# Norm scratch in PSUM, the context's norm first, and other banks for the feed-forward's opening, in a two-layer fp32 transformer kernel

## The chip, the cores and the metric

One core of a Trainium2 chip runs the whole program in one launch. The metric is the device time of that core in microseconds (us); lower is better.

## The reference, cut to what matters

Two layers over 512 latent tokens and 256 context tokens, 1024 features, fp32. Each layer has a mixer (layer 0: mLSTM heads and windowed attention; layer 1: global and neighbourhood attention) and a convolutional feed-forward, and in front of each stands a modulated RMS norm:

```python
def rms_norm(x, g):
    y = xf * lax.rsqrt(jnp.mean(xf * xf, axis=-1, keepdims=True) + EPS)
    return (y * g.astype(f32)).astype(x.dtype)

def modulate(x, g, shift, scale):
    return rms_norm(x, g) * (1 + scale) + shift

def conv_ffn(h, w_up, conv_w, conv_b, w_down):
    u = h @ w_up                                   # 1024 -> 2 x 2816
    u = depthwise_conv3(u, conv_w) + conv_b
    gate, val = jnp.split(u, 2, axis=-1)
    return (jax.nn.silu(gate) * val) @ w_down
```

Mixer and feed-forward are added to x through gates. Latents and context have their own shift, scale and gate. Of layer 1 only the latent stream is an output, so its second norm and its feed-forward see 512 tokens.

## The kernel before, in words

x lies transposed in SBUF: 8 tiles j of 128 features by 768 tokens (512 latent, 256 context). A matrix product is made from split operands: weight and activation are each rounded to a high half (fp32r, a faster matmul type) plus a low remainder, and three matmuls (high by high, high by low, low by high) add up in PSUM; `mm3` (L164 to L174) writes them out, `gemm_set` (L303) does the same with tokens on the output's partitions. Every weight block goes through `wchunk` (L138): SyncE issues a DMA of up to 512 KB into one of 4 "raw" buffers, ScalarE rounds it to `whi` (L145), GpSimd subtracts to get `wlo` (L146); there are 3 buffers of each.

PSUM has eight banks of 512 fp32 columns, handed out by tag (L69): "s" two buffers of two banks, "t" two of one bank, "mm" and "o" one each. `mmps` (L73) takes the tags in `mmtags` in turn. The order of instructions on each engine is fixed when the program is built: instructions are traced in program order and a list scheduler with a simulated timeline orders each engine's queue; on the chip each queue runs in that order and waits at semaphores.

A norm other than the first has these steps, on one stream of n tokens (512, or 256):

- behind each output tile of a projection, VectorE updates x (L1046 in `out_proj`, L1154 in the feed-forward's down product), ScalarE squares the new tile into an SBUF buffer `sq` (two buffers, L247), and VectorE adds it to `acc` (L248, both operands in SBUF)
- `norm_stat` (L250): matmuls by a column of ones sum `acc` over features into a "t" bank (L258); `rsqrt` (L120) computes 1/rms with twelve small VectorE instructions (L125 to L132), all but the first in SBUF; matmuls against the identity broadcast it to all partitions into another "t" bank (L265); ScalarE copies that to SBUF `rb` (L267)
- `norm_tile` (L271), for each of 8 j: VectorE scales x by weight and 1/rms into `ntmp` (four SBUF buffers, L279), ScalarE adds the shift and rounds to the high half (L281), VectorE makes the low half (L282). The halves are `hlh`, `hll` for latents and `hch`, `hcl` for context.

Three places have such norms. In `run` (L1166) layer 0's second norm: the second half of the output projection on latents, their norm, the same projection on the context, its norm, then `ffn`. At the end of `ffn` for layer 0 the last down product runs for latents, then for the context, and each stream's norm (layer 1's first) follows; `odd_mixer` then opens with a product by `W2` whose four latent token tiles run side by side in both "s" buffers (`wide`, L321). Layer 1's second norm treats the 512 latents as two halves of 256 with a projection each; the first half's high and low parts go to the context's tiles H[2], H[3], and DMAs move them later.

`ffn` (L1051) opens with the first four output tiles, (0,0), (0,1), (1,0), (1,1): for the first stream all four tiles, then for the second, so that TensorE has work while the second stream is normed. In layer 0 stream 0 is latents (512 columns), stream 1 context. Their banks are "s", "mm" with half of "o", "s", "t" with the other half of "o"; in layer 1 "s", "s", "mm", "o". The fourth tile's weights use spare buffers of later gate tiles.

Of the kernel before, what the change touches and what calls it, by code (L numbers as in the profile page):

```python
# [6 lines left out]
F32 = mybir.dt.float32  # L7
# [8 lines left out]
P = 128  # L16
# [13 lines left out]
NB0, NB1, NB2 = (2, 2), (2, 4), (2, 4)  # L30
# [13 lines left out]
class Net:  # L44
# [194 lines left out]
    def sq_acc(self, pool, acc, x, first, pool_add=False):  # L239

        nc = self.nc
        if first:
            nc.scalar.activation(acc, x, AF.Square)
        else:
            n = x.shape[-1]
            sq = pool.tile([P, 512], F32, tag="sq", bufs=self.nb[0], name=self.n("sq"))
            nc.scalar.activation(sq[:, :n], x, AF.Square)  # L247
            (nc.gpsimd if pool_add else nc.vector).tensor_tensor(acc, acc, sq[:, :n], op=ALU.add)  # L248

    def norm_stat(self, pool, *accs, tags=("t", "t")):  # L250
# [11 lines left out]
        for (acc, n), t0 in zip(accs, at):  # L262
# [3 lines left out]
            rb = pool.tile([P, 512], F32, tag="rb", bufs=2, name=self.n("rb"))  # L266
            nc.scalar.activation(rb[:, :n], bp[:, :n], AF.Copy)  # L267
            rbs.append(rb)
        return rbs

    def norm_tile(self, pool, l, i, j, X, rb, t0, n, s, hh, hl, o0):  # L271
# [3 lines left out]
        tm = pool.tile([P, 512], F32, tag="ntmp", bufs=self.nb[1], name=self.n("ntmp"))  # L275
        a, b, c = tm[:, :n], X[:, j, t0:t0 + n], rb[:, :n]
# [4 lines left out]
        nc.scalar.activation(hh[:, j, o0:o0 + n], tm[:, :n], AF.Identity, bias=sh)  # L281
        nc.vector.scalar_tensor_tensor(hl[:, j, o0:o0 + n], tm[:, :n], sh, hh[:, j, o0:o0 + n], op0=ALU.add, op1=ALU.subtract)  # L282

    def norm_apply(self, pool, l, i, X, acc, t0, n, s, hh, hl, o0):
        rb, = self.norm_stat(pool, (acc, n))
        for j in range(KT):
            self.norm_tile(pool, l, i, j, X, rb, t0, n, s, hh, hl, o0)
# [32 lines left out]

    def wide(self):  # L321

        s2 = [self.psum("s") for _ in range(2)]
        return [(t, s2[t // 2][:, t % 2 * 512:t % 2 * 512 + 512]) for t in range(NLT)]
# [291 lines left out]
    def start(self, X, H, pool, ev_gate, room):  # L616
# [19 lines left out]
        for i, (a, b) in enumerate(((0, LAT), (LAT, TOK))):  # L636
            got = set()
            for j in range(KT):
                h = int(i == 0 and j in (1, 3))
                self.sq_acc(pool, sums[i][h], X[:, j, a:b], h not in got, h)  # L640
                got.add(h)
            if len(got) > 1:
                nc.vector.tensor_tensor(sums[i][0], sums[i][0], sums[i][1], op=ALU.add)
            rbs += self.norm_stat(pool, (sums[i][0], b - a), tags=(("t", "t"), ("mm", "o"))[i])
# [4 lines left out]
        for j in range(KT):  # L649
            ada(j + AHEAD)  # L650
            for (t0, n, s) in ((0, LAT, 0), (LAT, CTX, 1)):
                self.norm_tile(pool, 0, 0, j, X, rbs[s], t0, n, s, H[2 * s], H[2 * s + 1], 0)
# [11 lines left out]
    def even_mixer(self, es):  # L664
# [26 lines left out]
        with ExitStack() as ns:  # L691
            self.nrm = self.pool("nrm0", ns)
            self.nb = NB0
# [165 lines left out]
    def odd_mixer(self, H, xd, es):  # L859
# [38 lines left out]
        self.mmtags = ["mm", "t"]  # L898
        wk = outer.tile([P, 2, 1024], F32R, tag="nq", name="wk")
        W2 = self.chunks(W[2], 256, self.K2)  # L900
        self.gemm_set(W2, 256, self.wide(), H, ev(ckv, 0, 1))
# [126 lines left out]
    def out_proj(self, l, ksel, xin, xout, streams, accs):  # L1028

        nc, d = self.nc, self.d  # L1030
        for jp in range(4):
# [8 lines left out]
            for jj in range(2):  # L1040
                j = 2 * jp + jj
                for i, (hh, hl, o0, n, t0, s) in enumerate(streams):
# [4 lines left out]
                    if accs is not None:  # L1047
                        self.sq_acc(self.nrm, accs[i], xs, j == 0)


    def ffn(self, l, X, H, T, tail, es, fin=None, work=None):  # L1051
# [6 lines left out]
        def banks(j, half):  # L1058

            if lat_only:  # L1060
                u = self.psum("s" if j != 1 else ("mm", "o")[half])[:, :LAT]
# [40 lines left out]
        for gi, (p0, p1) in enumerate(GROUPS):  # L1102
            G = []
            ready = {}
            if gi == 0:
                first = [(0, 0), (0, 1), (1, 0), (1, 1)]
                Ws = [weights(*f, spare=i == 3) for i, f in enumerate(first)]
                if lat_only:
                    us = [banks(*f) for f in first]
                else:  # L1110
                    o = self.psum("o")
                    us = [banks(0, 0), [self.psum("mm")[:, :LAT], o[:, :CTX]], banks(1, 0), [self.psum("t")[:, :LAT], o[:, CTX:]]]
                for i in range(2):
# [5 lines left out]
            for j in range(p0, p1):  # L1119
                cv = []  # L1120
                for half in range(2):
                    u = ready.get((j, half))
                    if u is None:
                        W = weights(j, half)
# [17 lines left out]
            for streams in passes:  # L1142
                for j in range(KT):
# [6 lines left out]
                    for o0, n, t0, s, acc in cut:  # L1150
# [4 lines left out]
                        if acc is not None:  # L1155
                            self.sq_acc(self.nrm, acc, xs, j == 0)
# [9 lines left out]
    def run(self):  # L1166
# [6 lines left out]
        self.nb = NB1  # L1173
# [3 lines left out]
        xj = lambda j: X[:, j, :]  # L1177
# [125 lines left out]
```

## Time and profile before, and how to read it

| | |
|---|---|
| time, median of 3 runs | 1817.64 us (1816.6 to 1818.77) |
| the profiled execution's own time | 1819.8 us |
| its span, first to last instruction | 1818.0 us |
| mean granted clock of TensorE | 0.985 |
| busy: TensorE, VectorE, ScalarE, GpSimd | 1713.1, 892.2, 659.0, 682.9 us |

In the profile PE is TensorE, DVE VectorE, ACT ScalarE, POOL GpSimd, SP SyncE. Times are us from the start of the span unless marked ns; L279 is line 279 of the kernel before; `out<-in` are the program's names; `x7` counts instructions. A row of waits names the engine and line that stood idle and the engine and line that released it. The granted clock is the share of full speed that TensorE was given.

### The profile page before, as it was taken

Reading aid. Unit: us, or ns where it says so; the run is one execution under the profiler, and the core shown is the slowest. Engines: PE = TensorE matmul, PEld = TensorE weight load, DVE = VectorE, ACT = ScalarE, POOL = GpSimd, SP = SyncE. Lnnn points to the kernel's source line nnn. Section 1 sums busy time; section 2 is a strip of 40 time slices with the busy share of each in tenths; the row PEclk is TensorE's granted clock in tenths of the full one; section 3 lists DMA queues with packets and bytes.
Section 4 is the critical chain, followed back from the end, with each engine's and each line's share of the span. In section 5 each row is a group of like instructions: output and inputs, shape, how many; then the busy total and the mean of one; then the engine's idle time right before and its main releaser. Section 6 shows DMA issues by size and latency. Waiting matters only on the chain.

```text
span 1818.0 us, 27843 instructions
## 1 busy us (share of the span) xinstructions
PE 1713.1 (94%) x11057; PEld 1461.1 (80%) x11057; DVE 892.2 (49%) x1897; ACT 659.0 (36%) x1145; POOL 682.9 (38%) x539
## 2 busy tenths in 40 slices
PE   4899998899899999999999988899989799999999
PEld 4679788788688888888788878789867788888887
DVE  6642458775853321333134477776266854143242
ACT  3422343553443311322123343365445444243341
POOL 2133226443422222222323353644374534443442
PEclk9999999999899999999999998999999899999999
DMA  8542431401323333332431242211242333323322
GB/s 294 177 171 70 155 130 52 132 22 36 105 70 105 128 105 128 105 125 99 136 129 55 73 163 70 71 42 36 73 128 74 124 98 102 93 92 86 113 86 77
DMA packets 62257, 187.62 MB, mean 103 GB/s; under 512 B 8048, under 2 KB 14320, under 8 KB 61872
## 3 DMA queue, kind: packets, MB, share of 16 engines
q1 hardware_dynamic: 62128, 185.85, 32.1%
q8 instruction: 87, 1.43, 0.3%
q14 instruction: 42, 0.34, 0.1%
HBM read 170.68 MB, written 4.39 MB: 96 GB/s over the span
## 4 chain that ended last, share of the span: by engine, by line
PE 81%; DVE 11%; ACT 2%; POOL 2%; DMA 2%; issue 1%; SPq 0%; DVEq 0%; ACTq 0%; POOLq 0%
PE s L170 11%; PE s L172 11%; PE s L174 11%; PE mm L170 3%; PE mm L172 3%; PE mm L174 3%; PE t L170 3%; PE o L603 3%; PE t L172 3%; PE t L174 3%; PE t L583 3%; PE o L170 2%; PE o L174 2%; PE o L172 2%; PE mm L310 2%; PE o L186 2%
## 5 line engine op out<-in xcount | busy, mean ns | idle before, releaser
L146 POOL TENSOR_TENSOR wlo<-raw,whi 128x1024 fp32r<-128x1024 f32 (+2 forms) x210 | 492.0, 2348 | 881.7 <-ACT whi L145 855.4
L145 ACT ACTIVATE whi<-raw 128x1024 fp32r<-128x1024 f32 (+2 forms) x210 | 214.2, 1025 | 503.7 <-PE s L172 179.0
L172 PE MATMUL s<-hll,whi 128*128 128x512 f32 (+1 forms) x704 | 275.9, 392 | 4.8 <-DVE hll L282 4.8
L170 PE MATMUL s<-hlh,whi 128*128 128x512 f32 (+1 forms) x704 | 277.2, 394 | 2.9 <-ACT hlh L281 2.6
L174 PE MATMUL s<-hlh,wlo 128*128 128x512 f32 (+1 forms) x704 | 275.5, 391 | 0.0
L1096 DVE SCALAR_TENSOR_TENSOR cv<-s,convw,cv 128x511 f32<-128x511 f32 x126 | 82.9, 658 | 330.1 <-ACT cv L1090 330.0
L170 PEld LDWEIGHTS s<-hlh,whi 128*128 128x128 f32 x704 | 132.6, 188 | 48.9 <-ACT whi L145 10.1
L172 PEld LDWEIGHTS s<-hll,whi 128*128 128x128 f32 x704 | 132.8, 189 | 33.8 <-DVE hll L282 5.4
L174 PEld LDWEIGHTS s<-hlh,wlo 128*128 128x128 f32 x704 | 132.6, 188 | 30.3 <-issue 0.8
L567 POOL TENSOR_SCALAR P<-P,sm 128x512 f32<-128x512 f32 (+3 forms) x112 | 84.0, 755 | 110.4 <-DVE sm L566 80.6
L172 PE MATMUL s<-hcl,whi 128*128 128x256 f32 x384 | 109.3, 285 | 5.6 <-DVE hcl L282 5.6
L174 PE MATMUL s<-hch,wlo 128*128 128x256 f32 x384 | 108.4, 282 | 0.0
L170 PE MATMUL s<-hch,whi 128*128 128x256 f32 x384 | 108.1, 282 | 0.0
L310 PE MATMUL mm<-whi,hlh 128*128 128x256 f32 x312 | 92.0, 295 | 4.0 <-ACT l1xt L876 2.4
L311 PE MATMUL mm<-wlo,hlh 128*128 128x256 f32 x312 | 90.1, 289 | 0.0
L312 PE MATMUL mm<-whi,hll 128*128 128x256 f32 x312 | 89.7, 287 | 0.0
L583 PE MATMUL t<-ident,P 128*128 128x128 f32 x496 | 77.9, 278 | 9.5 <-POOL E L964 4.7
L170 PE MATMUL t<-gh,whi 128*128 128x512 f32 (+1 forms) x221 | 85.8, 389 | 0.0
L1097 DVE SCALAR_TENSOR_TENSOR cv<-s,convw,cv 128x511 f32<-128x511 f32 x126 | 83.2, 661 | 4.5
L174 PE MATMUL t<-gh,wlo 128*128 128x512 f32 (+1 forms) x221 | 84.8, 384 | 0.0
L172 PE MATMUL t<-gl,whi 128*128 128x512 f32 (+1 forms) x221 | 84.8, 384 | 0.0
L172 PEld LDWEIGHTS s<-hcl,whi 128*128 128x128 f32 x384 | 73.3, 191 | 6.9 <-DVE hcl L282 6.0
(443 smaller groups left out, 4083.9 us busy)
## 6 DMA issues: line engine op xcount, KB each, us to landing
raw<-ada SPq DMA_DIRECT2D x96, 512.0 KB, 4.1
raw<-up SPq DMA_DIRECT2D x86, 512.0 KB, 3.7
raw<-down SPq DMA_DIRECT2D x40, 448.0 KB, 3.4
raw<-wout SPq DMA_DIRECT2D x24, 512.0 KB, 3.6
raw<-wodd SPq DMA_DIRECT2D x18, 512.0 KB, 3.6
raw<-down SPq DMA_DIRECT2D x16, 512.0 KB, 3.6
raw<-wtok SPq DMA_DIRECT2D x12, 512.0 KB, 3.8
raw<-wqk SPq DMA_DIRECT2D x8, 512.0 KB, 4.7
```

Source lines behind the costliest of these rows:

```text
L145: nc.scalar.activation(hi[:, :cols], raw[:, :cols], AF.Copy)
L146: nc.gpsimd.tensor_tensor(lo[:, :cols], raw[:, :cols], hi[:, :cols], op=ALU.subtract)
L170: nc.tensor.matmul(ps, wh, hh(k), start=(k == 0), stop=False, skip_group_check=True)
L172: nc.tensor.matmul(ps, wh, hl(k), start=False, stop=False, skip_group_check=True)
L174: nc.tensor.matmul(ps, wl, hh(k), start=False, stop=(k == nk - 1), skip_group_check=True)
L310: nc.tensor.matmul(ps[:, :ncols], a, W[k][0], start=(k == 0), stop=False, skip_group_check=True)
L311: nc.tensor.matmul(ps[:, :ncols], a, W[k][1], start=False, stop=False, skip_group_check=True)
L312: nc.tensor.matmul(ps[:, :ncols], b, W[k][0], start=False, stop=(k == KT - 1), skip_group_check=True)
L567: nc.gpsimd.tensor_scalar(Pt[:, :n], Pt[:, :n], sm, 0.0, op0=ALU.mult, op1=ALU.add)
L583: nc.tensor.transpose(tp[:, (b - g0) * P:(b - g0 + 1) * P], Pts[e][:, b * P:(b + 1) * P], self.ident)
L1096: nc.vector.scalar_tensor_tensor(y[:, a + 1:b], u[:, 0:n - 1], w(0), y[:, a + 1:b], op0=ALU.mult, op1=ALU.add)
L1097: nc.vector.scalar_tensor_tensor(y[:, a:b - 1], u[:, 1:n], w(2), y[:, a:b - 1], op0=ALU.mult, op1=ALU.add)
```

## The change

The changed functions serve all norms behind the first (the first keeps its SBUF buffers through `keep=True` and arguments). `slots(n)` takes one "s" buffer (two banks) and hands out slices of n columns in turn: two of 512 or four of 256. One such buffer holds the squares of a projection, another the scaled x of a norm, and 1/rms is read by VectorE from the "t" bank of the broadcast, with no copy. In layer 0 the context's projection and norm go ahead of the latents', and the feed-forward opens with three tiles, context stream first, in "mm" with half of "o", "t" with the other half, and "s"; the fourth tile's weights are still loaded there and used when its turn comes. In layer 1 the four opening tiles take "mm", "o", "s", "t". `wide` goes: the odd mixer's first product runs its latent token tiles one after another in banks "mm", "o", "t".

```diff
-    def sq_acc(self, pool, acc, x, first, pool_add=False):
+    def sq_acc(self, acc, x, first, sq, pool_add=False):
         nc = self.nc
         if first:
             nc.scalar.activation(acc, x, AF.Square)
         else:
-            n = x.shape[-1]
-            sq = pool.tile([P, 512], F32, tag="sq", bufs=self.nb[0], name=self.n("sq"))
-            nc.scalar.activation(sq[:, :n], x, AF.Square)
-            (nc.gpsimd if pool_add else nc.vector).tensor_tensor(acc, acc, sq[:, :n], op=ALU.add)
+            nc.scalar.activation(sq, x, AF.Square)
+            (nc.gpsimd if pool_add else nc.vector).tensor_tensor(acc, acc, sq, op=ALU.add)
+
+    def slots(self, n):
+        ps = self.psum("s")
+        return lambda j: ps[:, j % (1024 // n) * n:j % (1024 // n) * n + n]
...
-    def norm_stat(self, pool, *accs, tags=("t", "t")):
+    def norm_stat(self, pool, *accs, tags=("t", "t"), keep=False):
...
-            rb = pool.tile([P, 512], F32, tag="rb", bufs=2, name=self.n("rb"))
-            nc.scalar.activation(rb[:, :n], bp[:, :n], AF.Copy)
-            rbs.append(rb)
+            if keep:
+                rb = pool.tile([P, 512], F32, tag="rb", bufs=2, name=self.n("rb"))
+                nc.scalar.activation(rb[:, :n], bp[:, :n], AF.Copy)
+            rbs.append(rb if keep else bp)
         return rbs
-    def norm_tile(self, pool, l, i, j, X, rb, t0, n, s, hh, hl, o0):
+    def norm_tile(self, l, i, j, X, rb, t0, n, s, hh, hl, o0, tm):
         nc = self.nc
-        tm = pool.tile([P, 512], F32, tag="ntmp", bufs=self.nb[1], name=self.n("ntmp"))
-        a, b, c = tm[:, :n], X[:, j, t0:t0 + n], rb[:, :n]
+        a, b, c = tm, X[:, j, t0:t0 + n], rb[:, :n]
...
     def norm_apply(self, pool, l, i, X, acc, t0, n, s, hh, hl, o0):
         rb, = self.norm_stat(pool, (acc, n))
+        tm = self.slots(n)
         for j in range(KT):
-            self.norm_tile(pool, l, i, j, X, rb, t0, n, s, hh, hl, o0)
+            self.norm_tile(l, i, j, X, rb, t0, n, s, hh, hl, o0, tm(j))
...
-        self.mmtags = ["mm", "t"]
+        self.mmtags = ["mm", "o", "t"]
         wk = outer.tile([P, 2, 1024], F32R, tag="nq", name="wk")
         W2 = self.chunks(W[2], 256, self.K2)
-        self.gemm_set(W2, 256, self.wide(), H, ev(ckv, 0, 1))
+        for t in range(NLT):
+            self.gemm_set(W2, 256, [(t, self.mmps())], H, ev(ckv, 0, 1))
...
     def out_proj(self, l, ksel, xin, xout, streams, accs):
+        sqs = [self.slots(n) for _, _, _, n, _, _ in streams] if accs is not None else None
...
-                        self.sq_acc(self.nrm, accs[i], xs, j == 0)
+                        self.sq_acc(accs[i], xs, j == 0, sqs[i](j))
...
             if lat_only:
-                u = self.psum("s" if j != 1 else ("mm", "o")[half])[:, :LAT]
+                u = self.psum("s")[:, :LAT]
                 return [u[:, a:b] for a, b in segs] + [u]
...
                 Ws = [weights(*f, spare=i == 3) for i, f in enumerate(first)]
+                early = dict(zip(first, Ws))
                 if lat_only:
-                    us = [banks(*f) for f in first]
+                    us = [[u[:, a:b] for a, b in segs] + [u[:, :LAT]] for u in (self.psum(t) for t in ("mm", "o", "s", "t"))]
                 else:
                     o = self.psum("o")
-                    us = [banks(0, 0), [self.psum("mm")[:, :LAT], o[:, :CTX]], banks(1, 0), [self.psum("t")[:, :LAT], o[:, CTX:]]]
-                for i in range(2):
+                    us = [[self.psum("mm")[:, :LAT], o[:, :CTX]], [self.psum("t")[:, :LAT], o[:, CTX:]], banks(1, 0)]
+                for i in ((0, 1) if lat_only else (1, 0)):
                     for W, u in zip(Ws, us):
                         self.mm3(W, [stream(u, i)])
                 ready = dict(zip(first, us))
...
-                        W = weights(j, half)
+                        W = early.pop((j, half), None) or weights(j, half)
...
             for streams in passes:
+                sq = self.slots(streams[0][1]) if streams[0][4] is not None else None
...
-                            self.sq_acc(self.nrm, acc, xs, j == 0)
+                            self.sq_acc(acc, xs, j == 0, sq(j))
...
         al, ac = self.acc(LAT), self.acc(CTX)
         xj = lambda j: X[:, j, :]
+        self.out_proj(0, Bk, xj, xj, [cx], [ac])
+        H = self.htiles()
+        self.norm_apply(self.nrm, 0, 1, X, ac, LAT, CTX, 1, H[2], H[3], 0)
         self.out_proj(0, Bk, xj, xj, [lat], [al])
-        H = self.htiles()
         self.norm_apply(self.nrm, 0, 1, X, al, 0, LAT, 0, H[0], H[1], 0)
-        self.out_proj(0, Bk, xj, xj, [cx], [ac])
-        self.norm_apply(self.nrm, 0, 1, X, ac, LAT, CTX, 1, H[2], H[3], 0)
```

## Rows read from the trace of the kernel before

**Rows 1.** The page, part 1: busy us (share of the span) and instructions of each engine.

```profile
PE 1713.1 (94%) x11057; PEld 1461.1 (80%) x11057; DVE 892.2 (49%) x1897; ACT 659.0 (36%) x1145; POOL 682.9 (38%) x539
```

**Rows 2.** Waits of TensorE, three stretches: line waited for: us, times, longest.

```profile
PE s L172 <- DVE hll L282: 4.5, 1, 4.5
PE t L258 <- DVE acc L248: 2.8, 1, 2.8
PE t L265 <- DVE y L132: 1.8, 1, 1.8
...
PE s L312 <- DVE hll L282: 4.0, 2, 3.6
PE t L265 <- DVE y L132: 3.5, 1, 3.5
PE s L311 <- POOL wlo L146: 2.3, 1, 2.3
...
PE s L172 <- DVE hcl L282: 5.6, 2, 4.4
PE t L258 <- DVE acc L248: 3.5, 1, 3.5
PE s L170 <- ACT hlh L281: 1.5, 1, 1.5
```

**Rows 3.** Stretches: us, busy (instructions) by engine, granted clock, DMA share, GB/s.

```profile
440.00:535.00 95.00, 84.09 (x474) 72.72 (x473) 64.69 (x109) 39.59 (x59) 32.26 (x14) 0.95 0.23 73
1040.00:1125.00 85.00, 73.99 (x505) 68.69 (x504) 63.72 (x99) 32.53 (x53) 37.88 (x17) 0.94 0.37 118
1400.00:1500.00 100.00, 87.40 (x590) 79.72 (x590) 67.24 (x120) 44.15 (x74) 41.38 (x20) 0.93 0.31 102
1064.00:1068.00 4.00, 4.00 (x36) 4.00 (x36) 2.41 (x3) 1.64 (x3) 3.58 (x2) 1.00 1.03 346
```

**Rows 4.** VectorE by shape, 444:500 and 1408:1470: busy us, mean ns, idle before.

```profile
L248 DVE TENSOR_TENSOR acc<-acc,sq 128x512 f32<-128x512 f32 x7 | 11.9, 1697 | 2.0 <-ACT sq L247 1.1 <-ACT acc L243 0.7
L279 DVE SCALAR_TENSOR_TENSOR ntmp<-x,avec,rb 128x512 f32<-128x512 f32 x8 | 9.5, 1222 | 1.0 <-ACT rb L267 1.0
L282 DVE SCALAR_TENSOR_TENSOR hll<-ntmp,mod,hlh 128x512 fp32r<-128x512 f32 x8 | 8.3, 1055 | 0.0
...
L248 DVE TENSOR_TENSOR acc<-acc,sq 128x256 f32<-128x256 f32 x14 | 15.4, 1097 | 1.4 <-ACT sq L247 0.9
...
L282 DVE SCALAR_TENSOR_TENSOR hcl<-ntmp,mod,hch 128x256 fp32r<-128x256 f32 x8 | 7.8, 992 | 0.0
L282 DVE SCALAR_TENSOR_TENSOR hll<-ntmp,mod,hlh 128x256 fp32r<-128x256 f32 x8 | 3.4, 479 | 0.0
```

**Rows 5.** Timeline (start us, us), then one source line (min/median/max ns).

```profile
452.47 2.40 POOL L146 TENSOR_TENSOR wlo<-raw,whi 128x1024 fp32r<-128x1024 f32 x1 [4.73 <-ACT whi L145]
...
453.01 2.41 DVE L248 TENSOR_TENSOR acc<-acc,sq 128x512 f32<-128x512 f32 x1 [0.70 <-ACT acc L243]
...
456.01 0.68 DVE L248 TENSOR_TENSOR acc<-acc,sq 128x512 f32<-128x512 f32 x1
...
1418.03 0.41 DVE L248 TENSOR_TENSOR acc<-acc,sq 128x256 f32<-128x256 f32 x1
...
L1154 DVE SCALAR_TENSOR_TENSOR x<-t,mod,x x30: 468/751/752, 649.6 to 1814.8; 128x512 f32<-128x512 f32 x27, 128x256 f32<-128x256 f32 x3
```

**Rows 6.** 1/rms on VectorE: a group by shape in 1040:1125, then two timeline rows.

```profile
L127 DVE TENSOR_SCALAR y<-ms 128x4 int32<-128x4 int32 x1 | 1.8, 1844 | 0.0
...
1104.26 0.16 DVE L125 TENSOR_SCALAR ms<-t 128x2 f32<-128x2 f32 x1 [1.10 <-PE t L258]
...
1106.43 0.16 DVE L132 SCALAR_TENSOR_TENSOR y<-rt,y 128x2 f32<-128x2 f32 x1
```

**Rows 7.** Timeline of TensorE at layer 1's first broadcast.

```profile
1074.18 1.16 PE L265 MATMUL t<-ident,y 128*128 128x128 f32 x8 [3.54 <-DVE y L132]
1075.10 0.37 PE L170 MATMUL t<-gh,whi 128*128 128x256 f32 x1
```

More of the change, by code (lines that the diff above doesn't have):

```diff
@@ L29 @@
 WR, WH, RB0 = 4, 3, 2
-NB0, NB1, NB2 = (2, 2), (2, 4), (2, 4)
+NB0 = (2, 2)
 PB1, EB, PB0, PTB = 4, 2, 4, 4
@@ L280, in norm_tile @@
         sh = self.modcol(l, 3 * i, j, s)
-        nc.scalar.activation(hh[:, j, o0:o0 + n], tm[:, :n], AF.Identity, bias=sh)
-        nc.vector.scalar_tensor_tensor(hl[:, j, o0:o0 + n], tm[:, :n], sh, hh[:, j, o0:o0 + n], op0=ALU.add, op1=ALU.subtract)
+        nc.scalar.activation(hh[:, j, o0:o0 + n], tm, AF.Identity, bias=sh)
+        nc.vector.scalar_tensor_tensor(hl[:, j, o0:o0 + n], tm, sh, hh[:, j, o0:o0 + n], op0=ALU.add, op1=ALU.subtract)
     def norm_apply(self, pool, l, i, X, acc, t0, n, s, hh, hl, o0):
         rb, = self.norm_stat(pool, (acc, n))
+        tm = self.slots(n)
         for j in range(KT):
-            self.norm_tile(pool, l, i, j, X, rb, t0, n, s, hh, hl, o0)
+            self.norm_tile(l, i, j, X, rb, t0, n, s, hh, hl, o0, tm(j))
     def htiles(self):
@@ L319, in gemm_tok @@
             self.gemm_set(W, ncols, [(t, self.mmps())], H, evac)
-    def wide(self):
-        s2 = [self.psum("s") for _ in range(2)]
-        return [(t, s2[t // 2][:, t % 2 * 512:t % 2 * 512 + 512]) for t in range(NLT)]
     K2 = ((0, 4), (4, 8))
@@ L639, in start @@
                 h = int(i == 0 and j in (1, 3))
-                self.sq_acc(pool, sums[i][h], X[:, j, a:b], h not in got, h)
+                sq = pool.tile([P, 512], F32, tag="sq", bufs=NB0[0], name=self.n("sq")) if h in got else None
+                self.sq_acc(sums[i][h], X[:, j, a:b], h not in got, sq and sq[:, :b - a], h)
                 got.add(h)
@@ L643, in start @@
                 nc.vector.tensor_tensor(sums[i][0], sums[i][0], sums[i][1], op=ALU.add)
-            rbs += self.norm_stat(pool, (sums[i][0], b - a), tags=(("t", "t"), ("mm", "o"))[i])
+            rbs += self.norm_stat(pool, (sums[i][0], b - a), tags=(("t", "t"), ("mm", "o"))[i], keep=True)
         for j in range(AHEAD):
@@ L651, in start @@
             for (t0, n, s) in ((0, LAT, 0), (LAT, CTX, 1)):
-                self.norm_tile(pool, 0, 0, j, X, rbs[s], t0, n, s, H[2 * s], H[2 * s + 1], 0)
+                tm = pool.tile([P, 512], F32, tag="ntmp", bufs=NB0[1], name=self.n("ntmp"))
+                self.norm_tile(0, 0, j, X, rbs[s], t0, n, s, H[2 * s], H[2 * s + 1], 0, tm[:, :n])
             for t in range(NTT):
@@ L692, in even_mixer @@
             self.nrm = self.pool("nrm0", ns)
-            self.nb = NB0
             self.start(X, H, self.nrm, ev_gate, hs)
@@ L1172, in run @@
         self.nrm = self.pool("nrm1", ns)
-        self.nb = NB1
         self.mmtags = ["mm", "o", "t"]
@@ L1199, in run @@
         self.nrm = self.pool("nrm2", ns)
-        self.nb = NB2
         self.mmtags = ["mm", "o", "t"]
```

## The prediction, made before the changed kernel was run

> **What bounds the kernel now.** The page comes first: TensorE is busy for 94% of the span [rows 1], so most of the time is matrix work that this change leaves alone, and what it can win is TensorE's waiting and its slow clock at the three places where a norm stands between two matrix products. The waits of TensorE, asked for each of these stretches, give it: 9.1 us around layer 0's second norm (4.5 + 2.8 + 1.8), 9.8 us around layer 1's first (4.0 + 3.5 + 2.3), 10.6 us around layer 1's second (5.6 + 3.5 + 1.5), 29.5 us in all, and nearly all of it ends with a VectorE instruction of the norm [rows 2]. The stretches by engine show a second loss: the granted clock has a mean of 0.95, 0.94 and 0.93 there, against 1.00 in a stretch without waits [rows 3]. With two levels, 1.2 and 2.4 GHz, a mean of 0.95 over 95 us costs at most 0.05 x 95 = 4.8 us of full-speed work, the others 0.06 x 85 = 5.1 and 0.07 x 100 = 7.0, 16.9 us together; some of it fell on idle time and cost nothing. So 29.5 + 16.9 = 46.4 us is the most that can come back.
>
> Why is VectorE late? The groups by shape show it. Adding a 512-wide square takes 1697 ns in the mean, the scaling 1222, the low part 1055 in layer 0; the first is 680 ns when left alone [rows 4, 5]. The 256-wide low part takes 992 ns in layer 1's second norm for the first half of the tokens and 479 for the second, the same work [rows 4]. The timeline tells the two cases apart: the 2.41 us addition started while GpSimd made a low weight half (2.40 us from 452.47) and ended half a microsecond behind it; the next, with GpSimd idle, took 0.68. And thirty updates of x, the same two-tensor form but with the product read from PSUM, lie between 468 and 752 ns [rows 5], though GpSimd is busy for 38% of the span [rows 1]. So a VectorE instruction with both tensors in SBUF stands still behind GpSimd; one with a tensor in PSUM doesn't.
>
> **Part by part.** *Squares, scaled x and 1/rms in PSUM.* All three two-tensor instructions of a later norm get a PSUM operand. Against the unblocked prices (additions 0.68 at 512 and 0.41 at 256; scaling and low part 0.75, as the update of x, and 0.48) the blocked time is 7 x 1.02 + 8 x 0.47 + 8 x 0.31 = 13.4 us in layer 0, and in layer 1's second norm 14 x 0.69 + 8 x 0.51 = 13.7 without its scalings [rows 4, 5]. That is VectorE's time; TensorE gets back only what it waited for. Six copies of 1/rms by ScalarE go too, each between the broadcast and the first scaling; they stand inside the waits for the low and high parts and are not counted again.
>
> No row shows VectorE or ScalarE writing to PSUM. The nearest is the update of x, which reads it at the SBUF price (468 against 479 ns at 256) [rows 4, 5]; I take that price. The upper end is today's blocked mean of the scaling, 1222 ns, half a microsecond more for each of 8 tiles in layer 0 and in layer 1's first norm, and in proportion 0.3 for 16 tiles in the last: 4 + 4 + 5 = 13 us; the lower end is nothing, as no row shows a write below that price. The squares on ScalarE fit between two output tiles of TensorE even if they doubled: one tile of 256 is 12 matmuls of 4.00/36 = 0.111 us, 1.3 us [rows 3].
>
> Scaled x now has two 512-wide slots for four buffers, so a third scaling waits for the first low part. Behind it on VectorE stand low parts and updates of x, for whose banks TensorE waits. The rounding on ScalarE that lies between runs beside the next scaling, so I take 0 to 0.2 us a tile, at most 1.6 a norm, nothing where TensorE has other work.
>
> *Layer 0: context first.* Both projections read the same four 512 KB weight blocks, so SyncE's queue carries the same eight transfers in the same order, ScalarE the same roundings, GpSimd the same low halves; what moves is their pace. A block lasts 24 x 0.111 = 2.7 us in the context's turn, and GpSimd needs 2.40 [rows 3, 5]: it keeps up with 0.3 us to spare. The context's projection now comes first, when its last attention output is just being rounded, and the latent tiles that filled that gap stand behind it: 0 to 3 us, I take 1.5. Its norm is then covered by the latent projection, twice as many columns.
>
> What is late next is the latent norm: update, square, addition (three of about 0.7), 1/rms (twelve small instructions from 1104.26 to 1106.59, 2.3 us), two passes through TensorE (an estimate of 1 each), scaling and rounding (0.7 each), some 8 us [rows 5, 6]. Its cover is the opening of the feed-forward on the context, three tiles x 24 x 0.111 = 8.0 us. After that each k-slice gives TensorE 9 matmuls of 0.22, 2.0 us, and VectorE delivers one in two instructions of 0.7. So the 4.5 and 2.8 go, and about 2 of 9.1 us stay; with 3.5 us of clock and less the 1.5 above, 9 us come back. The fourth tile's matmuls only move behind the opening; its weights are loaded where they were, so no queue sees it.
>
> *Layer 1's first norm.* The 4.0 us for the low parts go. The 3.5 us before the broadcast stay: there 1/rms itself stands behind GpSimd (its second instruction took 1844 ns [rows 6]), and those small instructions keep both operands in SBUF. Of the 2.3 us for a low weight half I take half back. New is that the first product of the odd mixer goes tile by tile through single banks instead of four tiles side by side, so fewer matmuls can follow each slice: up to 2 tiles x 2.7 us = 5.4 lost if the other banks are held, nothing if slices come early; I take 1.5. With 2.5 us of clock that gives about 6.
>
> *Layer 1's second norm.* Two chains, each of the same form; the first half's projection and opening cover them, 11 us each. Of 10.6 us 8.5 go, and 4.5 of 7.0 us of clock, so 13.
>
> The sum is 9 + 6 + 13 = 28 us. The profiled execution took 1819.8 us (span 1818.0 and 1.8 around it), 2.2 above the median of 1817.64; the loss is the same in both, so I take it from the median: 1790.
>
> **The rivals.** *The wait moves to 1/rms* (0.17). Its twelve instructions stay blockable, TensorE runs denser, GpSimd with it, and the broadcast holds up TensorE's queue as it does now in layer 1. For it: the 3.5 and the 1844 ns [rows 2, 6]. Against it: in layer 0 that wait is only 1.8. If the three other exposed chains lose 3.5 us at the broadcast too and half of the clock's 10.5 us stays away, 28 - 10.5 - 5.5 = 12 us are left: 1806.
>
> *Slots of one bank shut each other out* (0.12). Four 256-wide slots lie in two banks. If the next scaling cannot start before the low part of its bank neighbour, a tile takes scaling, rounding and low part in a row, 3 x 0.48 = 1.4 us, where two VectorE instructions would do in 0.9: 0.5 x 8 tiles x 2 norms of layer 1 = 8 us, so 1798. The Trainium skill speaks for this one: its page "PSUM — Partial Sum Buffer", section "PSUM bank collisions raise a hardware error", wants any two engines kept off one bank at a time, whatever the address, and so a dependency between such neighbours; no row of before shows two engines at one bank in this way. By that rule the sum would be 20, without it 28.
>
> *The broadcast's bank blocks the products* (slower, 0.08). 1/rms now stays in a bank "t" until the last scaling. Tiles seem to get "t" in program order: a context tile of that bank starts at 1075.10, right behind the broadcast at 1074.18 for which TensorE had stood 3.5 us [rows 7]. If a "t" tile must wait for eight scalings and their neighbours (8 x 2 x 0.7 = 11 us at 512, as much at 256 with the other half's updates), TensorE stands once its tiles in "mm" and "o" are used up. It costs all that is won when four norms stall by 28 / 4 = 7 us each; at 8.5 us the time is 1824. Against it: two tiles of 2.7 us and the next product can go ahead.
>
> *Nothing moves* (0.05): if a PSUM result is blocked as an SBUF one is, only the copies go: 1817. The thirty unblocked updates speak against it [rows 5]. *More* (0.05): 39 us return and the time is 1779.
>
> **Numbers.** The forecast has 0.53. The range reaches from 1778 (nearly all of 46.4 without the 7 us of layer 1's broadcast and the early turn) to 1808 (the forecast with 13 us of dear writes and 5 of small stalls; it takes in the first two rivals). What a measurement can tell is 0.2%, 3.6 us. Faster: 0.53 + 0.17 + 0.12 + 0.05 = 0.87; within: 0.05; slower: 0.08.
>
> **What would show it.** Right: no square's addition above 0.8 us, scalings and low parts of 512 near 0.75 beside a busy GpSimd; TensorE's waits for the addition gone; granted clock at or above 0.97 in the three stretches. The order shows as context squares ahead of latent ones in layer 0. Wrong: additions or scalings still at 1 us and more; a wait of TensorE for the last scaling ahead of a tile in "t"; or longer waits for 1/rms, which would make it the first rival.

## The result, and the profile after

Four runs of the changed kernel have a median of 1796.49 us (1795.76 to 1797.83), four of the kernel before 1817.12 (1816.44 to 1818.77). The medians differ by 20.6 us, and their quotient is 0.9886. The ratio by which all kernels below are compared is an estimate with an interval of its own: 0.9875, 95% interval 0.9857 to 0.9893, which is 22.7 us. Forecast were 28, and 1790 us.

The span fell from 1818.0 to 1795.3 us. Where it went is read from the timeline, at rows that end one stretch and begin the next: the last attention output of layer 0, the first update of x in the feed-forward, the first one of its last group, layer 1's first scores, the first update of x in its last projection, and the first one of its feed-forward. Timeline rows of after (start us, us; line numbers of after, where additions are L246, scaling L282, rounding L284, low part L285):

```profile
446.81 0.42 DVE L612 TENSOR_TENSOR hcl<-o,hch 128x256 fp32r<-128x256 f32 x1 [0.96 <-ACT hch L611]
643.20 0.75 DVE L1158 SCALAR_TENSOR_TENSOR x<-t,mod,x 128x512 f32<-128x512 f32 x1 [5.04 <-PE t L174]
1026.60 0.75 DVE L1158 SCALAR_TENSOR_TENSOR x<-o,mod,x 128x512 f32<-128x512 f32 x1 [5.72 <-PE o L174]
1155.99 0.39 PE L882 MATMUL s<-K,Q 128*128 128x512 f32 x1
1396.76 0.48 DVE L1048 SCALAR_TENSOR_TENSOR x<-t,mod,xcq 128x256 f32<-128x256 f32 x1 [0.60 <-PE t L174]
1527.20 0.75 DVE L1158 SCALAR_TENSOR_TENSOR x<-mm,mod,x 128x512 f32<-128x512 f32 x1 [5.36 <-PE mm L174]
```

In before the same six starts are 445.65, 649.61, 1033.01, 1168.69, 1410.7 and 1549.81. The differences between neighbours, for one profiled execution of every kernel of this study (each is named and explained below), with its ratio to before from the timed runs:

| kernel | layer 0, second norm | layer 1, first norm | attention | layer 1, second norm | ratio, 95% |
|---|---|---|---|---|---|
| before | 204.0 | 135.7 | 242.0 | 139.1 | 1 |
| after | 196.4 | 129.4 | 240.8 | 130.4 | 0.9875, ±0.0018 |
| one slot | 197.1 | 130.9 | 240.9 | 131.8 | 0.9887, ±0.0021 |
| squares only | 198.6 | 133.5 | 242.2 | 133.2 | 0.9913, ±0.0019 |
| squares, narrow opening | 198.4 | 141.0 | 240.4 | 134.9 | 0.9983, ±0.0010 |
| scaled x in SBUF | 199.9 | 140.1 | 242.0 | 131.7 | 0.9950, ±0.0016 |
| 1/rms in SBUF | 200.6 | 139.7 | 239.7 | 134.2 | 0.9939, ±0.0022 |
| latents first | 201.3 | 129.9 | 242.4 | 132.7 | 0.9927, ±0.0014 |
| old opening | 197.1 | 129.2 | 240.4 | 130.2 | 0.9862, ±0.0023 |
| 1/rms computed in PSUM | 196.8 | 124.0 | 240.7 | 132.2 | 0.9845, ±0.0019 |
| that, two tiles in three norms | 197.9 | 123.2 | 240.8 | 129.2 | 0.9810, ±0.0025 |
| that, two tiles in layer 1 only | 198.1 | 121.9 | 240.5 | 128.8 | 0.9809, ±0.0014 |
| weight buffers | 197.3 | 131.1 | 240.8 | 135.6 | 0.9908, ±0.0014 |
| all together | 196.7 | 123.6 | 239.2 | 131.4 | 0.9836, ±0.0017 |

The stretch from the second row to the third (383.4 us) and the last one, from the sixth row to the end of the span (268 us), are the same in all. Kernels whose code doesn't differ in a stretch differ there by up to 3.2 us (attention: 239.2 in the last kernel of the table, 242.4 with latents first), and the first of the six rows starts anywhere between 441.0 and 448.9 us, so smaller differences are not read one by one. Before to after: 7.6 + 6.3 + 1.2 + 8.7 = 23.8 us, less 1.2 by which the first stretch began later.

VectorE did what was forecast. The page of after, part 1, then its groups by shape in 444:500 and 1400:1460 (busy us, mean ns, idle before), to be held against [rows 1, 4]:

```profile
PE 1707.4 (95%) x11057; PEld 1455.6 (81%) x11057; DVE 851.1 (47%) x1897; ACT 656.1 (37%) x1139; POOL 676.6 (38%) x539
```

```profile
L246 DVE TENSOR_TENSOR acc<-acc,s 128x512 f32<-128x512 f32 x7 | 4.8, 681 | 0.6 <-ACT s L245 0.5
L282 DVE SCALAR_TENSOR_TENSOR s<-x,avec,t 128x512 f32<-128x512 f32 x3 | 2.2, 749 | 0.0
...
L282 DVE SCALAR_TENSOR_TENSOR s<-x,avec,t 128x256 f32<-128x256 f32 x16 | 7.8, 488 | 0.8 <-PE t L268 0.4
L246 DVE TENSOR_TENSOR acc<-acc,s 128x256 f32<-128x256 f32 x13 | 5.5, 420 | 4.2 <-ACT s L245 4.0
L285 DVE SCALAR_TENSOR_TENSOR hll<-s,mod,hlh 128x256 fp32r<-128x256 f32 x8 | 3.9, 483 | 4.3 <-ACT hlh L284 4.3
```

Additions fell from 1697 to 681 ns and from 1097 to 420, scalings of 512 from 1222 to 749: none of these stands behind GpSimd any more, and a write to PSUM costs what one to SBUF does (749 ns against 740 in layer 0 of the kernel below that keeps scaled x in SBUF). Of the later norms only the small instructions of 1/rms still stand there, for up to 2.3 us. New is the last column: VectorE is free and waits 4.3 us for ScalarE's rounding. TensorE's waits in after, in 440:535, 1030:1120 and 1385:1485 (line waited for: us, times, longest), against [rows 2]:

```profile
PE o L170 <- ACT hch L284: 2.0, 4, 0.5
...
PE t L268 <- DVE y L132: 3.6, 2, 3.3
PE mm L314 <- ACT hlh L284: 2.4, 3, 1.0
...
PE mm L170 <- ACT hch L284: 1.4, 3, 0.6
PE o L174 <- POOL wlo L146: 1.4, 1, 1.4
PE s L174 <- POOL wlo L146: 1.3, 1, 1.3
PE o L170 <- ACT whi L145: 0.8, 1, 0.8
```

All waits for additions and nearly all for low parts are gone. In their place stand waits for the rounding, one per tile, and in layer 1's second norm for weights. The granted clock of the three stretches is 0.96, 0.96 and 1.00 against 0.95, 0.94 and 0.93 [rows 3] (stretch: us, busy and instructions by engine, granted clock, DMA share, GB/s):

```profile
440.00:535.00 95.00, 91.98 (x520) 77.79 (x519) 57.60 (x112) 40.22 (x60) 31.44 (x15) 0.96 0.29 95
1030.00:1120.00 90.00, 83.22 (x570) 77.09 (x569) 50.29 (x117) 35.01 (x58) 41.49 (x20) 0.96 0.39 125
1385.00:1485.00 100.00, 93.18 (x640) 82.66 (x639) 59.00 (x128) 49.49 (x82) 44.48 (x23) 1.00 0.36 116
```

### The profile page after: what moved, and what is told of

Its sections match the earlier page's. It is cut to its first block, busy times and chain, and to the rows that moved or that the text cites. A ratio compares the mean times of both kernels' runs of the same rounds, so it can differ in the third digit from the quotient of the medians.

```text
span 1795.3 us, 27798 instructions
## 1 busy us (share of the span) xinstructions
PE 1707.4 (95%) x11057; PEld 1455.6 (81%) x11057; DVE 851.1 (47%) x1897; ACT 656.1 (37%) x1139; POOL 676.6 (38%) x539
## 4 chain that ended last, share of the span: by engine, by line
PE 82%; DVE 8%; ACT 3%; issue 2%; DMA 2%; POOL 2%; SPq 0%; ACTq 0%; DVEq 0%; POOLq 0%
PE s L170 11%; PE s L174 11%; PE s L172 11%; PE mm L170 4%; PE mm L172 3%; PE mm L174 3%; PE t L170 3%; PE o L602 3%; PE t L172 3%; PE t L174 3%; PE t L582 3%; PE mm L314 2%; PE o L170 2%; PE o L172 2%; PE o L174 2%
## 5 line engine op out<-in xcount | busy, mean ns | idle before, releaser
L146 POOL TENSOR_TENSOR wlo<-raw,whi 128x1024 fp32r<-128x1024 f32 (+3 forms) x210 | 486.0, 2319 | 865.3 <-ACT whi L145 813.9
L145 ACT ACTIVATE whi<-raw 128x1024 fp32r<-128x1024 f32 (+3 forms) x210 | 214.7, 1026 | 513.5 <-PE s L172 180.9
L172 PE MATMUL s<-hll,whi 128*128 128x512 f32 (+1 forms) x696 | 272.3, 391 | 0.0
L1137 ACT ACTIVATE gh<-cv 128x768 fp32r<-128x768 f32 (+1 forms) x44 | 32.5, 739 | 122.8 <-DVE cv L1136 122.8
```

The lines of the kernel that those rows point to most:

```text
L145: nc.scalar.activation(hi[:, :cols], raw[:, :cols], AF.Copy)
L146: nc.gpsimd.tensor_tensor(lo[:, :cols], raw[:, :cols], hi[:, :cols], op=ALU.subtract)
L172: nc.tensor.matmul(ps, wh, hl(k), start=False, stop=False, skip_group_check=True)
```

## Experiments

**Do the slots do anything?** Every later norm uses the first slot of its tile alone.

```diff
-        return lambda j: ps[:, j % (1024 // n) * n:j % (1024 // n) * n + n]
+        return lambda j: ps[:, :n]
```

> The kernel after, but every later norm's squares and scaled x use the first slot of their two-bank PSUM tile only, never the second to fourth. Theory W (the program lets one holder at a time into the whole two-bank tile, so the slots are worth nothing): no change, 1796.5 us within 1.5, and scalings of one norm still 1.55 us apart for 256 columns and about 2.3 us for 512. Theory B, as in the prediction's rival (only slots of one bank shut each other out, 512-wide slots lie in two banks and overlap): the two norms over 512 columns lose the overlap, 0.5 to 0.8 us a tile, so 4 to 6 us where it is on the path, 1799 to 1803 us.

The ratio is 0.9887 against 0.9875, intervals overlapping: no difference. VectorE's timeline of after, first 512-wide tiles, then 256-wide:

```profile
1085.68 0.75 DVE L282 SCALAR_TENSOR_TENSOR s<-x,avec,t 128x512 f32<-128x512 f32 x1
1087.19 0.75 DVE L285 SCALAR_TENSOR_TENSOR hll<-s,mod,hlh 128x512 fp32r<-128x512 f32 x1
1087.97 0.76 DVE L282 SCALAR_TENSOR_TENSOR s<-x,avec,t 128x512 f32<-128x512 f32 x1
...
1430.77 0.49 DVE L282 SCALAR_TENSOR_TENSOR s<-x,avec,t 128x256 f32<-128x256 f32 x1
1431.80 0.48 DVE L285 SCALAR_TENSOR_TENSOR hll<-s,mod,hlh 128x256 fp32r<-128x256 f32 x1 [0.54 <-ACT hlh L284]
1432.32 0.49 DVE L282 SCALAR_TENSOR_TENSOR s<-x,avec,t 128x256 f32<-128x256 f32 x1
```

and of the kernel with one slot:

```profile
1083.44 0.76 DVE L282 SCALAR_TENSOR_TENSOR s<-x,avec,t 128x512 f32<-128x512 f32 x1
1084.95 0.75 DVE L285 SCALAR_TENSOR_TENSOR hll<-s,mod,hlh 128x512 fp32r<-128x512 f32 x1
1085.74 0.76 DVE L282 SCALAR_TENSOR_TENSOR s<-x,avec,t 128x512 f32<-128x512 f32 x1
```

The period is 2.3 us in both (1087.97 - 1085.68 and 1085.74 - 1083.44), 1.55 at 256: a scaling follows the low part of the tile before it, also where their slots lie in different banks. Theory W holds.

**One part alone.** The kernel before, with its squares in PSUM and nothing else.

```diff
+            if sq is None:
+                sq = pool.tile([P, 512], F32, tag="sq", bufs=self.nb[0], name=self.n("sq"))
...
-                        self.sq_acc(self.nrm, accs[i], xs, j == 0)
+                        self.sq_acc(self.nrm, accs[i], xs, j == 0, sq=sqs[i](j))
```

> The kernel before with one part of the change alone: the squares of the later norms go to a two-bank PSUM tile; scaled x, 1/rms, the order in layer 0 and the openings stay as they were. Theory: additions fall to 0.41 and 0.69 us as after (26 us less of VectorE), but the path's end is mostly set by what follows them, so 3 to 7 us of time, ratio 0.996 to 0.998. Rival (the additions were the main wait): 10 us or more, ratio 0.9945 or less, with the layer 1 second norm's half (8 updates of x from first to last 7.7 us as after instead of 13.1) the largest piece.

0.9913: 16 us, more than the theory allowed; it is the rival's size. Layer 0's stretch gains 5.4 us, layer 1's two 2.2 and 5.9. So the additions alone, with the old opening kept, bring most of what the whole change brings. In the same kernel, the opening of layer 1's mixer is then made as in after:

```diff
-        self.gemm_set(W2, 256, self.wide(), H, ev(ckv, 0, 1))
+        for t in range(NLT):
+            self.gemm_set(W2, 256, [(t, self.mmps())], H, ev(ckv, 0, 1))
```

> The kernel of the run with the squares alone in PSUM, but the odd mixer opens tile by tile on three one-bank accumulators, as after, instead of four tiles side by side in the two two-bank tiles. Theory (the change paid for its PSUM tiles with this opening, and this is why layer 1's first norm got slower than in the kernel before as soon as only one of scaled x and 1/rms lay in PSUM): the stretch from the feed-forward's last group to layer 1's first scores grows by 4 to 6 us from 133.5 us, ratio 0.9935 to 0.9950. Rival (the opening is free): the stretch stays within 1.5 us, ratio 0.990 to 0.9925.

Layer 1's first norm grows by 7.5 us (133.5 to 141.0), more than the theory's 4 to 6, and the ratio to 0.9983, outside both ranges. That is some 13 us; what goes beyond the 7.5 is not explained. TensorE's waits in 1040:1125 of this kernel:

```profile
PE mm L316 <- DVE x L1163: 8.4, 1, 8.4
PE t L271 <- DVE y L132: 6.0, 2, 3.5
PE mm L318 <- DVE hll L288: 2.1, 1, 2.1
```

A product of the mixer needs the bank "mm", and the context's update of x that frees it stands behind blocked norm instructions on VectorE. With four tiles side by side in "s" that bank was needed later: the same wait was 2.6 us in the kernel before this one.

**Scaled x back in SBUF**, all else as after:

```diff
-        tm = self.slots(n)
         for j in range(KT):
-            self.norm_tile(l, i, j, X, rb, t0, n, s, hh, hl, o0, tm(j))
+            tm = pool.tile([P, 512], F32, tag="ntmp", bufs=4, name=self.n("ntmp"))
+            self.norm_tile(l, i, j, X, rb, t0, n, s, hh, hl, o0, tm[:, :n])
```

> The kernel after, but the scaled x of the later norms goes to four buffers of 512 in SBUF, as in the kernel before; squares and 1/rms stay in PSUM. Theory W (the one-at-a-time PSUM tile is what the norms now cost): a norm of 8 tiles of 256 falls from 12.4 us to about 8 us, TensorE's waits for hch in layer 0 (2.0 us, with the granted clock at 0.5 behind them) and in layer 1's second norm (1.4 us) go, 1789 to 1793 us. Rival S (low parts with both tensors in SBUF stand behind GpSimd again, up to 2 us each, and the scaling with 1/rms in PSUM is not blocked): the low parts' longest is above 2 us, waits for hll or hcl come back, and the time is 1796 to 1802 us.

0.9950, about 14 us worse than after: the rival's signs came, and a loss beyond its range. Low parts beside GpSimd, on the timeline of this kernel (two instructions in GpSimd's row), and TensorE's wait for them:

```profile
1081.62 5.15 POOL L146 TENSOR_TENSOR wlo<-raw,whi 128x1024 fp32r<-128x1024 f32 x2 [1.73 <-ACT whi L145]
1082.18 2.37 DVE L285 SCALAR_TENSOR_TENSOR hll<-ntmp,mod,hlh 128x512 fp32r<-128x512 f32 x1
...
PE mm L316 <- DVE hll L285: 4.1, 3, 2.1
```

Not all of this is GpSimd. In layer 1's first norm the scaling writes its 512 columns in transposed order, in steps of eight (the `rearrange` in `norm_tile`). Into SBUF that took 1218 ns in the mean of eight, though 1/rms was read from PSUM, and about 1.1 us each in the two scalings below, where GpSimd had nothing to do (it sat idle for the 7.19 us ahead of 1074.48); into PSUM the same eight took 752 ns in after.

```profile
1069.59 2.15 DVE L282 SCALAR_TENSOR_TENSOR ntmp<-x,avec,t 128x512 f32<-128x512 f32 x2 [1.49 <-PE t L268]
...
1074.48 5.42 POOL L146 TENSOR_TENSOR wlo<-raw,whi 128x896 fp32r<-128x896 f32 x2 [7.19 <-ACT whi L145]
```

**1/rms copied to SBUF again**, so that the scaling reads two SBUF tensors and writes PSUM:

```diff
-        rb, = self.norm_stat(pool, (acc, n))
+        rb, = self.norm_stat(pool, (acc, n), keep=True)
```

> The kernel after, but the later norms copy 1/rms to SBUF again (one copy of ScalarE a norm) and scale from there; squares and scaled x stay in PSUM. The scaling then reads two tensors in SBUF and writes PSUM. Theory P1 (one tensor in PSUM is enough, the output too): no scaling above 0.8 us, the copies cost 0.5 to 0.7 us a norm of which little shows, ratio to the kernel before 0.987 to 0.989. Theory P2 (only what is read counts): scalings of up to 2.6 us beside GpSimd come back, above all in layer 1's first norm, ratio 0.990 to 0.995.

0.9939: theory P2. The scaling's line (min/median/max ns), on the timeline a scaling that started 0.31 us into a GpSimd subtraction (two in its row), and one of TensorE's waits in 1030:1120:

```profile
L282 DVE SCALAR_TENSOR_TENSOR s<-x,avec,rb x48: 485/494/2654, 468.1 to 1453.2; 128x256 f32<-128x256 f32 x32, 128x512 f32<-128x512 f32 x16
...
1076.35 5.22 POOL L146 TENSOR_TENSOR wlo<-raw,whi 128x1024 fp32r<-128x1024 f32 x2 [0.55 <-ACT whi L145]
1076.66 2.65 DVE L282 SCALAR_TENSOR_TENSOR s<-x,avec,rb 128x512 f32<-128x512 f32 x1
...
PE t L314 <- DVE ckv L874: 5.1, 1, 5.1
```

For the blocking it doesn't matter where the result goes; what is read does. Six scalings took over 1 us. But they don't account for the whole loss. Layer 1's first norm is 10.3 us longer than in after, and of its scalings only the one above was blocked, for 1.9 us. TensorE stood 5.1 us there for a copy that empties a bank "t" of the product by `W2` (`ckv`, L874). The scheduler put the first of these copies behind all eight of the context's scalings on VectorE's queue (1105.61 us); in after it stands behind the second (1095.05), and the wait is 0.4. The same late copies are in the two other kernels with the narrow opening and about 140 us in this stretch, scaled x in SBUF and squares with the narrow opening. How much of the 10 us is blocking and how much this order, no run separates.

**Order and opening of layer 0.** Latents first again, then (alone) the opening in the old four banks:

```diff
-                for i in ((0, 1) if lat_only else (1, 0)):
+                for i in range(2):
...
+        self.out_proj(0, Bk, xj, xj, [lat], [al])
         H = self.htiles()
-        self.norm_apply(self.nrm, 0, 1, X, ac, LAT, CTX, 1, H[2], H[3], 0)
-        self.out_proj(0, Bk, xj, xj, [lat], [al])
         self.norm_apply(self.nrm, 0, 1, X, al, 0, LAT, 0, H[0], H[1], 0)
+        self.out_proj(0, Bk, xj, xj, [cx], [ac])
+        self.norm_apply(self.nrm, 0, 1, X, ac, LAT, CTX, 1, H[2], H[3], 0)
```

> The kernel after, but layer 0's second norm and the opening of its feed-forward take the latents first again, as before; the rest is kept. If the order gave most of layer 0's gain (6.4 us by the first update of x in its feed-forward): 1800 to 1803 us, all of the loss ahead of that update. If the gain came from PSUM operands and the context's early turn only moves the stall (four waits of 0.5 us for hch instead of waits for hlh): 1795 to 1798 us.

```diff
-                    us = [[self.psum("mm")[:, :LAT], o[:, :CTX]], [self.psum("t")[:, :LAT], o[:, CTX:]], banks(1, 0)]
+                    us = [banks(0, 0), [self.psum("mm")[:, :LAT], o[:, :CTX]], banks(1, 0), [self.psum("t")[:, :LAT], o[:, CTX:]]]
```

> The kernel after, but layer 0's feed-forward opens with four tiles in the banks of before (two of them two-bank tiles that squares and scaled x hold too) instead of three in other banks. Theory: the opening's first tile has to wait until the latents' squares or the context norm let go of a two-bank tile, TensorE waits 3 to 8 us there, ratio 0.989 to 0.992. Rival (they are free in time): ratio 0.987 to 0.988, no wait for a tile.

The old order costs 4.9 us in layer 0 (201.3 against 196.4) and 9 in the ratio; the other 4 lie in stretches that the edit leaves alone and stay unexplained. The old opening costs nothing that can be measured (0.9862; the theory of a wait for its first tile was wrong).

**The wait for 1/rms.** Its small instructions read one operand in the PSUM bank of the sums:

```diff
+        if tp is not None:
+            ms, t = tp[:, 8:8 + n], tp[:, 16:16 + n]
...
+                nc.vector.scalar_tensor_tensor(t, ms, -0.5, y, op0=ALU.mult, op1=ALU.mult)
+                nc.vector.tensor_tensor(t, t, y, op=ALU.mult)
```

> The kernel after, but in the norms over rows of x the small instructions of 1/rms read one operand in PSUM each (mean square and product in the bank of the sums, two products in another order). Theory P (these instructions stand behind GpSimd only because both operands lie in SBUF): none of them above 0.4 us in the later norms (after: up to 2.3 us), TensorE's 3.3 us wait for the broadcast in layer 1's first norm falls below 1 us and the clock's fall behind it shrinks, 1790 to 1794 us. Rival (the broadcast waits for the squares' last addition and the GpSimd work is not the cause): the waits stay, 1796 to 1797 us.

Theory P, in size too: 0.9845, and layer 1's first norm 5.4 us shorter. First 1/rms of that norm in after (groups by shape), then in this kernel, with TensorE's wait for the broadcast in 1023:1113 (lines are 7 higher):

```profile
L132 DVE SCALAR_TENSOR_TENSOR y<-rt,y 128x4 f32<-128x4 f32 x3 | 2.4, 803 | 0.1
L131 DVE SCALAR_TENSOR_TENSOR rt<-rt,ms 128x4 f32<-128x4 f32 x3 | 2.2, 750 | 0.1
```

```profile
L139 DVE SCALAR_TENSOR_TENSOR y<-t,y 128x4 f32<-128x4 f32 x3 | 0.5, 162 | 0.1
L134 DVE SCALAR_TENSOR_TENSOR t<-t,y 128x4 f32<-128x4 f32 x3 | 0.5, 167 | 0.1
...
PE t L275 <- DVE y L139: 0.3, 1, 0.3
```

**Two tiles by turns.** On top of it, scaled x alternates between "s" and a "t" bank:

```diff
         tm = self.slots(n)
+        if alt:
+            even, odd = tm, self.psum("t")
+            tm = lambda j: odd[:, :n] if j % 2 else even(j // 2)
```

with two accumulators, "mm" and "o", for the product beside it; first in three norms, then in layer 1 only.

> The kernel of the run with 1/rms in PSUM, and in three norms (context of layer 0's second, latents of layer 1's first, first half of layer 1's second) scaled x goes by turns to the two-bank tile and to a one-bank tile of its own; the projection beside them has two accumulators instead of three. Theory W (one holder at a time in a tile is what spaces the scalings): period of two scalings below 2.2 us for 256 columns instead of 3.1, TensorE's waits for hch (1.7 us in layer 0, 1.1 in layer 1) and for hlh (1.5) mostly gone and the low clock behind them too, ratio 0.981 to 0.983. Rival (two accumulators are too few): waits for updates of x on mm and o appear and eat it, ratio 0.985 to 0.988.

> The kernel of the run with two tiles by turns, but layer 0's context norm goes back to the one two-bank tile and its projection to three accumulators; the two norms of layer 1 keep their two tiles. In that run layer 0's stretch had got no shorter (197.9 us against 196.8 with one tile), with a new wait of 1.5 us for an update of x. Theory (two accumulators cost in layer 0 what the faster norm gives): layer 0's stretch about 196.8 us, ratio 0.979 to 0.981. Rival (the stretch's length was chance): ratio 0.981 to 0.983.

Both give 0.981, so theory W holds for layer 1. Layer 0 gained nothing in the first kernel; for the second, which undoes the edit there, the rival holds: its stretch stayed at 198.1. VectorE's timeline of the second, layer 1's second norm, and TensorE's waits in 1381:1481 with the stretch (us, busy by engine, granted clock, DMA share, GB/s):

```profile
1413.62 0.48 DVE L289 SCALAR_TENSOR_TENSOR t<-x,avec,t 128x256 f32<-128x256 f32 x1
1414.01 0.48 DVE L292 SCALAR_TENSOR_TENSOR hcl<-s,mod,hch 128x256 fp32r<-128x256 f32 x1
1414.40 0.41 DVE L253 TENSOR_TENSOR acc<-acc,s 128x256 f32<-128x256 f32 x1
1414.73 0.48 DVE L289 SCALAR_TENSOR_TENSOR s<-x,avec,t 128x256 f32<-128x256 f32 x1
1415.12 0.47 DVE L292 SCALAR_TENSOR_TENSOR hcl<-t,mod,hch 128x256 fp32r<-128x256 f32 x1
...
PE t L275 <- DVE y L139: 2.5, 1, 2.5
...
1381.00:1481.00 100.00, 95.41 (x637) 85.55 (x634) 56.80 (x122) 48.67 (x80) 44.97 (x22) 0.98 0.36 116
```

A tile now takes 1.1 us (1413.62 to 1414.73), an addition included, and VectorE has no gap. The weight waits of 1.4 and 0.8 us are gone without any edit to weights; a wait of 2.5 for 1/rms, unblocked but with nothing beside it, took their place.

**The weights.** After, with two more buffers for rounded and low weight parts in layer 1's last projection; then this on top of the best kernel.

```diff
+                keep = (lambda tag: self.nrm.tile([P, 1024], F32R, tag="n" + tag, bufs=2, name=self.n(tag))) if l == 1 and accs is not None and jp % 2 else None
```

> The kernel after, but every second weight piece of layer 1's last projection has buffers of its own (two more rounded and two more low-part buffers, in the SBUF that squares, scaled x and 1/rms left free). In after TensorE waits in layer 1's second norm 1.4 us for a low part of the weights and 0.8 us for a rounded piece. Theory B (the pieces come late because their buffers are held by products still to run): these two waits go, 1 to 2 us, ratio 0.986 to 0.987. Rival G (GpSimd's 2.4 us a piece is itself the limit): the waits stay or move, ratio 0.987 to 0.988.

> All that helped, together: 1/rms with an operand in PSUM, two tiles by turns in layer 1's two norms, more weight buffers in layer 1's last projection. If the gains add: ratio 0.978 to 0.980. If the weights are bound by GpSimd or the waits only move: as the run without the weight buffers, 0.979 to 0.982.

Neither foresaw this: 0.9908, some 6 us slower than after, and 0.9836 instead of 0.9809. The kernel with the buffers, timeline, TensorE's waits in 1385:1490 and a window:

```profile
1415.98 1.26 POOL L146 TENSOR_TENSOR wlo<-raw,whi 128x512 fp32r<-128x512 f32 x1 [1.23 <-ACT whi L145]
1416.06 1.19 DVE L131 SCALAR_TENSOR_TENSOR rt<-rt,ms 128x2 f32<-128x2 f32 x1
...
PE t L268 <- DVE y L132: 2.9, 1, 2.9
PE o L174 <- POOL wlo L146: 0.6, 1, 0.6
...
1428.00:1440.00 12.00, 11.48 (x64) 10.65 (x65) 8.15 (x28) 3.33 (x8) 0.00 (x0) 0.72 0.56 202
```

The waits for weights shrank from 2.2 to 0.6 us in the projection, but GpSimd now works on the feed-forward's weights while 1/rms is computed. One of the instructions of 1/rms takes 1.19 us beside it, another 0.80, where 0.16 and 0.17 are enough: that is 1.7 of the 2.9 us for which TensorE waits in one piece. Ten microseconds later the granted clock is 0.72, in a window where after had 1.00. The blocking is thus shown as a part of the loss only. In the best kernel 1/rms can't be blocked, and there the buffers cost something too, though TensorE's wait for 1/rms is 1.9 us with them and 2.5 without; why stays open.

## Why the prediction was right, and where it was not

- *Bound and mechanism*: right. Instructions with both tensors in SBUF stand behind GpSimd, and all three kinds that were given a tensor to read in PSUM are freed. One word was too wide: "one with a tensor in PSUM doesn't" holds for tensors read, not for the one written (2654 ns in the run with 1/rms in SBUF). The Trainium skill, page "SBUF — State Buffer", section "SBUF: two separate sides", names a VectorE instruction "with two SBUF inputs" as one that stands until GpSimd is done if it comes second, and names no output; the trace agrees.
- *Price of PSUM writes*: right, 488 and 749 ns where 480 and 750 were taken; the upper end of 13 us is void.
- *Layer 0, 9 us*: 7.6. The order is worth 5, as its sign was argued. "About 2 of 9.1 us stay" came true in size by luck: the 2.0 us are waits for the rounding of the context's norm, which the forecast had called covered, and not for the latents' norm. The 1.5 us for the context's early turn can't be read: the stretch's start lies between 441.0 and 448.9 us in kernels with the same code before it.
- *Layer 1's first norm, 6 us*: 6.3, but not term by term. The broadcast's 3.5 us stayed (3.3), and its cause is shown by the run that removed it. The 4.0 for low parts fell to 0.4 and the 2.3 for weights went whole, but 2.4 for the rounding came in. The tile-by-tile opening was taken at 1.5. It cost 7.5 in the kernel where it was tried alone, with VectorE still blocked; what it costs in after, where the waits of that product come to 3.2 us (2.4 + 0.4 + 0.4), no run separates.
- *Layer 1's second norm, 13 us*: 8.7, and 1.2 ahead of it that is no more than chance. "Of 10.6 us 8.5 go" failed as a term: the three waits that it counts did go, but others came. All of TensorE's waits in the stretch sum to 12.6 us in before and 6.2 in after, 3.5 of them for weights and 1.4 for roundings, so 6.4 went. That leaves 8.7 - 6.4 = 2.3 us for the clock, where 4.5 were taken, though the clock was at 1.00.
- *The term that was most wrong* is the slots: "0 to 0.2 us a tile, at most 1.6 a norm". The slots are no buffers at all. A 256-wide tile took 1.55 us instead of about 0.9, 5 us a norm on VectorE; the two-tile kernel, which undoes it in layer 1, ran 0.9845 - 0.9809 = 0.36% faster, 6.5 us with an uncertainty of about 4. That is the size by which the forecast was too good, 5 to 7 us. (It changed the accumulators as well.)

So the mechanism of the second rival came true beside the forecast's, and its time, 1798, lies nearer to 1796.5 than the forecast does; the range had been drawn to take it in. It was wider than priced: slots in two banks waited too, and one slot ran like two, so it is this program that orders whole tiles. The Trainium skill, page "PSUM — Partial Sum Buffer", section "PSUM bank collisions raise a hardware error", asks for semaphores by bank (or quadrant of a bank); the order in this trace goes further, over both banks of a tile. The first rival (more wait at 1/rms in the other norms) didn't come in this kernel, where those waits fell to 0.3 us or less outside layer 1's first norm, but it did with more weight buffers. No wait in after was for a bank "t" that 1/rms held, the third rival's sign. Of the signs named, additions, prices and order came as written; the clock of at least 0.97 came in one stretch of three.

The experiments end at a kernel that beats both: 1/rms computed in PSUM and two tiles by turns in layer 1, 0.9809 (0.9796 to 0.9823).

## What to carry to other kernels

When VectorE stands behind GpSimd, look at what every instruction of the chain reads. With one link left in SBUF (scaled x or 1/rms) the kernel lost 12 to 14 us of the 23, a part of it perhaps through the order in which VectorE's copies were then queued: compare the queues too, since an edit moves instructions that it doesn't name. Count PSUM scratch in tiles that the program orders separately, not in slots of one tile, and price what the scratch displaces; here that was an opening whose loss cost 7.5 us while VectorE was still blocked. And an engine that gets ahead, as GpSimd with more buffers, can land beside a short chain that nobody had protected.

## What was not expected of the hardware

- For two-tensor instructions of VectorE only what is read decided whether they waited for GpSimd: one that writes PSUM from two SBUF tensors took up to 2654 ns instead of 760. Instructions of 1/rms with a single tensor, from SBUF to SBUF, stood too (L128, 2331 ns in after where 170 is usual).
- A transposed write of 512 columns, in steps of eight, took about 1.1 us into SBUF with GpSimd idle and 0.75 into PSUM.
- The granted clock is not told by the sum of the waits or by the longest one alone. After 6.2 us of waits in 100 us, none over 1.4, it stayed at 1.00 in after. With more weight buffers 8.9 us, 2.9 of them in one piece, stand beside 0.97 in 105 us and 0.72 in 1428:1440. And in layer 0 of after 2.7 us of waits, none over 0.5, stand beside 0.96 in 95 us: behind four of them within five microseconds it was 0.50 in 488:492.
- ScalarE's squares of 512 took 597 ns into PSUM (42 squares of the later norms, 14 of this width) and 626 into SBUF (the first norm, the same execution). The Trainium skill, page "ScalarE: Activation LUTs", section "Step-by-step: what each stage is for", calls PSUM the faster port for ScalarE; the trace agrees.
